# Head-unit accumulators of a projection stream: two PSUM banks moved from the stream's pool to the side pool

## The chip, the cores and the metric

The kernel runs on one core of one Trainium2 chip. The metric is device time in microseconds (us); three runs of the kernel before gave 840.37 us as their median, from 839.36 to 842.27.

## The reference, cut to what matters

One layer of a recurrent decoder is computed for 256 prompt positions and 8 sample positions, together T = 264 columns. All projections are one product `p = x @ w_in` with d_model 2048; its first 2048 columns ("qk") pass through a causal convolution of width 4 and a SiLU:

```
p = x @ w_in
(qk_pre, a_v, a_i, a_f, a_o, a_z, b_q, b_k, b_v, b_g, b_z, g_a, g_b) = _split_cols(p)
ext = jnp.concatenate([conv_buf.astype(qk_pre.dtype), qk_pre], axis=1)
conv = conv_b
for j in range(CONV_W):
    conv = conv + ext[:, j:j + L] * conv_w[j]
qk = jax.nn.silu(conv)
```

The rest (an mLSTM branch, a GLA branch, their norms and gates, two branch projections, the output projection and a LayerNorm) follows later in the stream and is not touched here.

## The kernel before

**Units.** The weight columns are cut into units of 128 columns. Units 0 to 15 are the qk columns, then come the gate columns ("small") and all other projections, the branch projections and the output projection. A unit is a product of 16 blocks of 128 rows, and each block takes three matmuls of 128x264: high part of x by high part of the weight (L218), low part of x by high part of the weight (L219), high part of x by low part of the weight (L221). A unit thus takes 48 matmuls, which accumulate in one PSUM bank.

**Weights.** A unit's weights come as two pieces of 512 KB. In this text pieces are counted from the first unit behind the head: unit 3 takes pieces 0 and 1, unit 4 takes 2 and 3, unit 5 takes 4 and 5, unit 6 takes 6 and 7. A piece is loaded by SP's queue into one of four `raw` buffers (L182), cast by ACT into one of five `hi` buffers (L204), and subtracted by DVE into one of five `lo` buffers (L205). The cast of piece n needs the `hi` buffer of piece n-5 back from TensorE, and the load of piece n the `raw` buffer of piece n-4 back from DVE.

**The head.** Units 0 to 2 (HU = 3) are computed together, block by block, while x itself arrives (nine steps of one or two blocks), so they hold three accumulators at once. From unit 3 on, the units run one after the other.

**Banks.** PSUM's eight banks are two pools: `ps_m` with three, which the stream's units take in turn (tile name `mm`), and `ps_s` with five, which everything else takes in turn (tile name `sd`). A unit's bank is taken from the one that used it three allocations earlier, and its first matmul waits until that tile has been read for the last time.

**Eviction of a qk unit** (`e_qk`, number c): ACT scales the accumulator into `cacc` (L255), DVE adds three shifted products of the same accumulator to it (L257, widths 255, 254, 253, with L259 for the sample columns between), ACT copies eleven columns to `co` (L260) and takes a sigmoid (L261), DVE multiplies (L262). L260 is the last reader of the bank.

**Order.** TensorE's order is that of the code. On ACT and DVE a scheduler sets the order from priorities and its own times, so a dependence that changes in the code can move instructions there; each engine then runs its list in order. Behind unit 4's weights SP also loads five constants (L1162), `wgu_sb` among them, which ACT casts to `wgh` (L301) and DVE turns into `wgr` (L302).

Of the kernel before, what the change touches and what calls it, by code (L numbers as in the profile page):

```python
# [13 lines left out]
F32 = mybir.dt.float32  # L14
# [9 lines left out]
T = L + NB  # L24
# [24 lines left out]
HU = 3  # L49
# [35 lines left out]
def body(ctx, tc, xT, whead, wbig, wsmall, par, cmask, lmask, rowc, gate, wgu, cT, sT, nst, cst, lnr,  # L85
# [11 lines left out]
    ps_m = ctx.enter_context(tc.tile_pool(name="ps_m", bufs=3, space=PSUM))  # L97
# [3 lines left out]
    def t4(shape, name, dt=F32):  # L101
        return b4.tile(shape, dt, tag="b4", name=name)
# [21 lines left out]
    def side_ps():  # L124
        return ps_s.tile([128, 512], F32, tag="sd", name="sd")
# [44 lines left out]
    def load_raw():  # L170

        i = nxt["dma"]
        if i >= len(pieces):
            return
        r = wraw_p.tile([128, KR, 128], F32, tag="raw", name="raw")
        o = 0
        while i < len(pieces) and o + pieces[i][2] <= KR:
            n, k, m, bi = pieces[i]
            w = 128 if bi is not None else SMALL
            src = wbig[bi] if bi is not None else wsmall  # L180
            raws[i] = r[:, o:o + m, 0:w]
            nc.sync.dma_start(out=raws[i], in_=src[:, k:k + m, :])  # L182
            o += m
            i += 1
        nxt["dma"] = i

    def cast_piece():
        i = nxt["cast"]
        while nxt["dma"] <= i:
            load_raw()  # L190
        n, k, m, bi = pieces[i]
        nxt["cast"] += 1
        r = raws.pop(i)
        h = whi_p.tile([128, KR, 128], F32R, tag="hi", name="hi")[:, 0:m]
        if bi is None:
            w = SMALL
            A.copy(out=h[:, :, 0:w], in_=r)
            V.tensor_tensor(out=h[:, :, w:2 * w], in0=r, in1=f(h[:, :, 0:w]), op=ALU.subtract)
            for q in range(m):
                his[n, k + q] = h[:, q, 0:2 * w]  # L200
            return
        lo = wlo_p.tile([128, KR, 128], F32R, tag="lo", name="lo")[:, 0:m]
        with tc.high_priority(offset=PRIO):
            A.copy(out=h, in_=r)  # L204
            V.tensor_tensor(out=lo, in0=r, in1=f(h), op=ALU.subtract)  # L205
        for q in range(m):
            his[n, k + q], los[n, k + q] = h[:, q], lo[:, q]

    def split(hi, lo, src):
        A.copy(out=hi, in_=src)  # L210
        V.tensor_tensor(out=lo, in0=src, in1=f(hi), op=ALU.subtract)

    def products(out, n, k, rhs, start, stop, base=0):

        small = UN[n][0] == "small"
        wh = his[n, k]
        rh, rl = rhs(k - base)
        PE.matmul(out, lhsT=wh, rhs=rh, start=start, stop=False)  # L218
        PE.matmul(out, lhsT=wh, rhs=rl, start=False, stop=small and stop)  # L219
        if not small:  # L220
            PE.matmul(out, lhsT=los[n, k], rhs=rh, start=False, stop=stop)  # L221

    def group(n, k0, k1, rhs, base=0):

        ps = ps_m.tile([128, 512], F32, tag="mm", name="mm")
        out = ps[0:2 * SMALL if UN[n][0] == "small" else 128, 0:T]
        for k in range(k0, k1):
            products(out, n, k, rhs, k == k0, k == k1 - 1, base)
        return ps[:, 0:T]
# [346 lines left out]
    def e_plain(ps, j, key, scale=None):  # L576
        if j == 0:
            st[key] = t4([128, H, T], key)
        A.activation(out=st[key][:, j, :], in_=ps, func=AF.Copy, scale=1.0 if scale is None else scale)
        if j == 3:  # L580
            st[key + "_done"] = True
# [270 lines left out]
    def e_pab(pa, pb, j):  # L852
        g = gtiles[j // 2]
        i = 2 * (j % 2)
        ga, gb = g[:, i, :], g[:, i + 1, :]
        V.tensor_tensor(out=ga, in0=ga, in1=pa, op=ALU.mult)
        V.tensor_tensor(out=gb, in0=gb, in1=pb, op=ALU.mult)
        V.tensor_tensor(out=ga, in0=ga, in1=gb, op=ALU.add)
        split(mh.t(j), ml.t(j), ga)
# [4 lines left out]
    def ln_pre(j):  # L864

        xt = tmp.tile([128, T], F32, tag="t1", name="xt", bufs=T1_BUFS)
        G.tensor_tensor(out=xt, in0=f(x_hi[j // 4][:, j % 4, :]), in1=f(x_lo[j // 4][:, j % 4, :]), op=ALU.add)
        ln["x", j] = xt
# [41 lines left out]
    def ln_shift(j):  # L910

        xt = ln["x", j]
        V.scalar_tensor_tensor(out=xt, in0=xt, scalar=ALPHA, in1=ln["c"], op0=ALU.mult, op1=ALU.subtract)
# [145 lines left out]
    def add(g, front=False):  # L1059
        side.insert(0, g) if front else side.append(g)  # L1060
# [52 lines left out]
    with tc.manual_schedule(engines=MANUAL):  # L1113
        V.memset(ones, 1.0)
        warm = side_ps()
        head = [(side_ps() if u == 0 else ps_m.tile([128, 512], F32, tag="mm", name="mm"))[:, 0:T] for u in range(HU)]
        V.memset(inv256, 1.0 / 256.0)
        V.memset(eps_c, EPS)
        V.memset(one_c, 1.0)
        for _ in range(8):  # L1120
            PE.matmul(warm[:, 0:128], lhsT=ones, rhs=ones, start=True, stop=True)
        k0 = 0
        for m in HEAD:
            k1, i, o = k0 + m, k0 // 4, k0 % 4
            xr = t4([128, m, T], "xr")
            nc.sync.dma_start(out=xr, in_=xT[:, k0:k1, :])
            wr, wh, wl = (p.tile([128, KR, 128], dt, tag=t, name=t)[:, 0:HU * m].rearrange("p (k u) c -> p k u c", u=HU)
                          for p, dt, t in ((wraw_p, F32, "raw"), (whi_p, F32R, "hi"), (wlo_p, F32R, "lo")))
            nc.sync.dma_start(out=wr, in_=whead[:, k0:k1])
            split(x_hi[i][:, o:o + m], x_lo[i][:, o:o + m], xr)  # L1130
            split(wh, wl, wr)
            for u in range(HU):
                for k in range(k0, k1):
                    his[u, k], los[u, k] = wh[:, k - k0, u], wl[:, k - k0, u]
                    products(head[u], u, k, x_rhs, k == 0, k == KT - 1)
            k0 = k1
        nc.sync.dma_start(out=par_sb, in_=par)
        nc.sync.dma_start(out=cst_sb, in_=cst)
        for n, (kind, j) in enumerate(UN):
            st['n'] = n  # L1140
            while nxt["cast"] < min(last.get(n, -1) + 1 + LA, len(pieces)):
                cast_piece()
                while nxt["dma"] < min(nxt["cast"] + RAW_BUFS - 1, len(pieces)):
                    load_raw()
            if kind == "pab":
                pa = group(n, 0, 8, lambda k: (st["yah"].t(k), st["yal"].t(k)))
                pb = group(n, 8, 16, lambda k: (st["ybh"].t(k), st["ybl"].t(k)), base=8)
                e_pab(pa, pb, j)
            elif kind == "out":
                ln_pre(j)  # L1150
                if j >= 8:
                    ln_shift(j)
                ps = group(n, 0, 16, lambda k: (mh.t(k), ml.t(k)))
                e_out(ps, j)
            else:
                ps = head[n] if n < HU else group(n, 0, 16, x_rhs)
                if n == 0:
                    g_conv_prep()
                if n == 4:
                    V.tensor_copy(out=im_sb, in_=ident)  # L1160
                    for dst, src in ((gate_sb, gate), (wgu_sb[64:112], wgu), (rc_sb, rowc), (cm_sb, cmask), (lm_sb, lmask)):
                        nc.sync.dma_start(out=dst, in_=src)  # L1162
                if kind == "qk":
                    for _ in e_qk(ps, j):
                        pass
                elif kind == "small":
                    add(g_gates(ps), True)
                elif kind == "av":
                    e_v(ps, j, "avt", "avd")
                elif kind == "bv":  # L1170
                    e_v(ps, j, "bvt", "bvd")
                elif kind == "bq":
                    e_plain(ps, j, "gq", Q_SCALE)
                elif kind == "bk":
                    e_plain(ps, j, "gk")
                elif kind in ("ao", "az"):
                    e_raw(ps, 2 * j + (kind == "az"), "ozr", 4, g_oz)
                elif kind == "bz":
                    e_raw(ps, j, "bzr", 4, g_bz)
                elif kind in ("ga", "gb"):  # L1180
                    e_raw(ps, 2 * j + (kind == "gb"), "gr", 4, g_g)
            pump(BUDGET)
            if kind == "gb" and j == 15:
                drain()
        ln_final()
# [136 lines left out]
```

## Time and profile before

| | us |
|---|---|
| median of three runs (range) | 840.37 (839.36 to 842.27) |
| the profiled execution | 837.3 |
| its span, first to last instruction | 835.5 |
| TensorE busy in it | 819.5 (98%) |
| DVE busy | 595.0 (71%) |
| ACT busy | 446.5 (53%) |

A busy share is a mean over the whole span; matmuls are pipelined, so a matmul's length in a row (0.28 us) is more than the distance to the next one (0.12 us). What an engine waited for is told by the waits, and the lists of instructions in order of time show where it did.

### The profile page before, as it was taken

The numbers are of one execution on the slowest core, as the hardware profiler recorded it, in microseconds if no ns is written. First come the engines' busy times: TensorE is split into PE (matmuls) and PEld (weight loads), VectorE is DVE, ScalarE is ACT, GpSimd is POOL, SyncE is SP. The second block draws the span as 40 slices with busy tenths as digits, with TensorE's granted clock in tenths as the row PEclk, the third lists the DMA queues.
The fourth block names the chain that finished last, engine by engine and source line by source line (L and its number), as shares of the span: only waits on it lengthen the run. The fifth ranks groups of instructions, "written<-read, shape, count | busy, mean of one in ns | idle before, by whom it ended". The sixth has DMA issues, their size and how long they took to land.

```text
span 835.5 us, 16720 instructions
## 1 busy us (share of the span) xinstructions
PE 819.5 (98%) x6762; PEld 809.9 (97%) x6762; DVE 595.0 (71%) x976; ACT 446.5 (53%) x675; POOL 44.6 (5%) x75
## 2 busy tenths in 40 slices
PE   8799999999999999999999999999999999999996
PEld 8799999999999999999999999999999999999995
DVE  6777667655667787867667997798845777666962
ACT  6555467546455564554546866566544444444633
POOL 0000000000000000001000000012000000000311
PEclk9999999999999999999999999999999999999999
DMA  8756565768759985588888679977655565576513
GB/s 308 253 167 185 158 195 169 202 205 262 247 160 315 310 309 188 200 285 285 278 264 300 200 263 339 296 276 227 197 181 180 183 187 179 180 252 205 186 42 105
DMA packets 56406, 186.39 MB, mean 223 GB/s; under 512 B 8404, under 2 KB 9880, under 8 KB 56328
## 3 DMA queue, kind: packets, MB, share of 16 engines
q1 hardware_dynamic: 52200, 170.90, 62.9%
q0 software_dynamic: 4128, 14.42, 4.5%
q8 instruction: 53, 0.87, 0.4%
q14 instruction: 25, 0.20, 0.1%
HBM read 168.58 MB, written 16.71 MB: 222 GB/s over the span
## 4 chain that ended last, share of the span: by engine, by line
PE 95%; DVE 2%; DMA 2%; ACT 1%; issue 0%; SPq 0%; ACTq 0%; POOLq 0%; POOL 0%; DVEq 0%
PE mm L218 29%; PE mm L219 29%; PE mm L221 29%; DMA gak<-rows_d 1%; PE sd L704 1%; PE sd L466 1%; DMA raw<-whead 1%; PE sd L425 1%; DVE lo L205 1%; PE sd L406 0%; PE sd L440 0%; PE sd L755 0%; PE sd L998 0%; PE sd L221 0%; PE sd L966 0%
## 5 line engine op out<-in xcount | busy, mean ns | idle before, releaser
L218 PE MATMUL mm<-xh,hi 128*128 128x264 f32 (+1 forms) x1536 | 441.1, 288 | 5.3 <-ACT co L260 5.3
L219 PE MATMUL mm<-xl,hi 128*128 128x264 f32 (+1 forms) x1536 | 435.3, 284 | 0.0
L221 PE MATMUL mm<-xh,lo 128*128 128x264 f32 x1520 | 431.0, 284 | 0.0
L204 ACT CAST hi<-raw 128x1024 fp32r<-128x1024 f32 x250 | 261.4, 1047 | 279.3 <-PE mm L219 239.6
L205 DVE TENSOR_TENSOR lo<-raw,hi 128x1024 fp32r<-128x1024 f32 x250 | 307.1, 1230 | 115.0 <-ACT hi L204 110.7
L218 PEld LDWEIGHTS mm<-xh,hi 128*128 128x128 f32 (+1 forms) x1536 | 289.7, 189 | 6.6 <-ACT co L260 5.5
L219 PEld LDWEIGHTS mm<-xl,hi 128*128 128x128 f32 (+1 forms) x1536 | 289.9, 189 | 0.2
L221 PEld LDWEIGHTS mm<-xh,lo 128*128 128x128 f32 x1520 | 285.7, 188 | 0.0
L218 PE MATMUL mm<-mh,hi 128*128 128x264 f32 x256 | 72.7, 284 | 0.0
L221 PE MATMUL mm<-mh,lo 128*128 128x264 f32 x256 | 72.6, 284 | 0.0
L219 PE MATMUL mm<-ml,hi 128*128 128x264 f32 x256 | 72.4, 283 | 0.0
L219 PEld LDWEIGHTS mm<-ml,hi 128*128 128x128 f32 x256 | 48.2, 188 | 0.0
L218 PEld LDWEIGHTS mm<-mh,hi 128*128 128x128 f32 x256 | 48.1, 188 | 0.0
L568 DVE SCALAR_TENSOR_TENSOR cch<-kq,avd,cch 128x256 f32<-128x256 f32 x64 | 29.2, 482 | 26.6 <-DMA kq<-kq_d 24.4
L221 PEld LDWEIGHTS mm<-mh,lo 128*128 128x128 f32 x256 | 48.0, 187 | 0.0
L553 ACT ACTIVATE cch<-cch,decb 128x512 f32<-128x512 f32 x32 | 21.6, 717 | 28.5 <-DMA cch<-cT 28.5
L219 PE MATMUL mm<-ybl,hi 128*128 128x264 f32 x128 | 36.4, 284 | 0.0
L218 PE MATMUL mm<-ybh,hi 128*128 128x264 f32 x128 | 36.4, 284 | 0.0
L218 PE MATMUL mm<-yah,hi 128*128 128x264 f32 x128 | 36.3, 284 | 0.0
L219 PE MATMUL mm<-yal,hi 128*128 128x264 f32 x128 | 36.3, 284 | 0.0
L221 PE MATMUL mm<-yah,lo 128*128 128x264 f32 x128 | 36.2, 283 | 0.0
L221 PE MATMUL mm<-ybh,lo 128*128 128x264 f32 x128 | 36.2, 283 | 0.0
(330 smaller groups left out, 854.3 us busy)
## 6 DMA issues: line engine op xcount, KB each, us to landing
raw<-wbig SPq DMA_DIRECT2D x250, 512.0 KB, 4.7
cch<-cT SPq DMA_DIRECT2D x16, 512.0 KB, 6.1
kq<-kq_d SPq DMA_DIRECT2D x16, 512.0 KB, 7.3
sC<-cch POOLq DMA_DIRECT2D x16, 512.0 KB, 4.9
sch<-sT SPq DMA_DIRECT2D x8, 512.0 KB, 8.5
gak<-rows_d SPq DMA_DIRECT2D x8, 512.0 KB, 7.5
sS<-sch POOLq DMA_DIRECT2D x8, 512.0 KB, 6.9
raw<-whead SPq DMA_DIRECT2D x7, 384.0 KB, 5.5
```

What stands on the lines that cost most here:

```text
L204: A.copy(out=h, in_=r)
L205: V.tensor_tensor(out=lo, in0=r, in1=f(h), op=ALU.subtract)
L218: PE.matmul(out, lhsT=wh, rhs=rh, start=start, stop=False)
L219: PE.matmul(out, lhsT=wh, rhs=rl, start=False, stop=small and stop)
L221: PE.matmul(out, lhsT=los[n, k], rhs=rh, start=False, stop=stop)
L425: PE.matmul(S[:, o:o + n], lhsT=kT.t(2 * h + d)[:, s0:s0 + 128], rhs=qT.t(2 * h + d)[:, t0:t0 + n], start=(d == 0), stop=(d == 1))
L466: PE.matmul(CN[:, 0:VC], lhsT=kw[:, s, d * 128:d * 128 + 128], rhs=vt[h // 2][:, s, h % 2, :], start=(s == 0), stop=(s == 1))
L553: A.activation(out=chunks[i][:, b], in_=chunks[i][:, b], func=AF.Copy, scale=decb[:, h, b0 + b:b0 + b + 1])
L568: V.scalar_tensor_tensor(out=c[:, b, e], in0=r[:, 0, b], scalar=avd[:, j, b0 + b:b0 + b + 1], in1=c[:, b, e], op0=ALU.mult, op1=ALU.add)
L704: PE.matmul(pl[s0:s0 + m, 4 * hf + h, n0:n0 + w].rearrange("p (n s) -> p n s", s=hs), lhsT=K[:, h, hf * 128 + s0:hf * 128 + s0 + m], rhs=r ...
```

## The change

All three accumulators of the head units are taken from the side pool `ps_s`; before, unit 0's was, and those of units 1 and 2 were from `ps_m`.

```diff
-        head = [(side_ps() if u == 0 else ps_m.tile([128, 512], F32, tag="mm", name="mm"))[:, 0:T] for u in range(HU)]
+        head = [side_ps()[:, 0:T] for u in range(HU)]
```

Matmuls, loads and computations are the same in number and size. The lists of TensorE, SP and POOL keep their order; on TensorE only the tile under units 1 and 2 has another name (`sd_108`, `sd_109` for `mm_108`, `mm_109`). Before, the allocations in `ps_m` were those two and then units 3, 4, 5, 6 (`mm_433`, `mm_504`, `mm_582`, `mm_653`), so unit 4 took unit 1's bank, unit 5 unit 2's and unit 6 unit 3's. Now units 3, 4 and 5 take three fresh banks, and unit 6 takes unit 3's as before.

On ACT the scheduler moves casts. From the cast of piece 6 on, before and then now (`hi_498` is piece 6, `hi_570` 7, `hi_576` 8, `hi_641` 9, `hi_647` 10; the three L260 read the banks of units 1, 2 and 3 for the last time):

```order
L204 CAST hi_498<-raw_425 128x1024
L260 COPY co_388<-mm_108 128x11
L261 ACTIVATE csg_402<-cacc_401 128x264
L255 ACTIVATE cacc_411<-mm_109,par_sb_84 128x264
L260 COPY co_388<-mm_109 128x11
L261 ACTIVATE csg_412<-cacc_411 128x264
L255 ACTIVATE cacc_482<-mm_433,par_sb_84 128x264
L301 CAST wgh_1478<-wgu_sb_89 48x512
L204 CAST hi_570<-raw_431 128x1024
L260 COPY co_388<-mm_433 128x11
```

```order
L204 CAST hi_570<-raw_431 128x1024
L260 COPY co_388<-sd_108 128x11
L261 ACTIVATE csg_402<-cacc_401 128x264
L255 ACTIVATE cacc_411<-sd_109,par_sb_84 128x264
L204 CAST hi_576<-raw_496 128x1024
L260 COPY co_388<-sd_109 128x11
L261 ACTIVATE csg_412<-cacc_411 128x264
L255 ACTIVATE cacc_482<-mm_433,par_sb_84 128x264
L301 CAST wgh_1478<-wgu_sb_89 48x512
L204 CAST hi_641<-raw_502 128x1024
L204 CAST hi_647<-raw_574 128x1024
L260 COPY co_388<-mm_433 128x11
```

The casts of pieces 7 to 10 stand earlier among the evictions: the last reader of unit 3's bank stood behind the cast of piece 7, and stands behind that of piece 10 now.

On DVE, around the eviction of unit 3 (`mm_433` is its bank, `cacc_482` its result), before and then now:

```order
L257 SCALAR_TENSOR_TENSOR cacc_482<-mm_433,par_sb_84,cacc_482 128x255
L259 TENSOR_TENSOR cacc_482<-cacc_482,dtap_382 128x8
L302 SCALAR_TENSOR_TENSOR wgr_1479<-wgh_1478,par_sb_84,wgu_sb_89 48x512
L257 SCALAR_TENSOR_TENSOR cacc_482<-mm_433,par_sb_84,cacc_482 128x254
L257 SCALAR_TENSOR_TENSOR cacc_482<-mm_433,par_sb_84,cacc_482 128x253
L205 TENSOR_TENSOR lo_571<-raw_431,hi_570 128x1024
```

```order
L302 SCALAR_TENSOR_TENSOR wgr_1479<-wgh_1478,par_sb_84,wgu_sb_89 48x512
L257 SCALAR_TENSOR_TENSOR cacc_482<-mm_433,par_sb_84,cacc_482 128x254
L205 TENSOR_TENSOR lo_642<-raw_502,hi_641 128x1024
L257 SCALAR_TENSOR_TENSOR cacc_482<-mm_433,par_sb_84,cacc_482 128x253
L205 TENSOR_TENSOR lo_648<-raw_574,hi_647 128x1024
```

Before, the two L257 of this unit followed each other behind L302; now the subtraction of piece 9 (`lo_642`) stands between them. Some fifteen rows further on the lists of ACT and DVE are again those of before, to their ends.

## Rows read from the trace of the kernel before

**Rows 1.** The page: busy us, share and count of TensorE; chain by engine.

```profile
PE 819.5 (98%) x6762; PEld 809.9 (97%) x6762; DVE 595.0 (71%) x976; ACT 446.5 (53%) x675; POOL 44.6 (5%) x75
...
PE 95%; DVE 2%; DMA 2%; ACT 1%; issue 0%; SPq 0%; ACTq 0%; POOLq 0%; POOL 0%; DVEq 0%
```

**Rows 2.** Waits of TensorE, whole span: total us, times, longest us.

```profile
PE mm L218 <- ACT co L260: 5.3, 1, 5.3
PE sd L218 <- ACT hi L210: 1.4, 2, 0.9
...
PE sd L644 <- DVE ns L637: 0.3, 1, 0.3
```

**Rows 3.** Timeline of TensorE: start us, length us, instruction, idle before it.

```profile
9.48 0.39 PE L218 MATMUL sd<-xh,hi 128*128 128x264 f32 x1 [0.88 <-ACT hi L210]
...
25.67 0.28 PE L218 MATMUL mm<-xh,hi 128*128 128x264 f32 x1
...
31.35 0.28 PE L221 MATMUL mm<-xh,lo 128*128 128x264 f32 x1
36.93 0.59 PE L218 MATMUL mm<-xh,hi 128*128 128x264 f32 x1 [5.29 <-ACT co L260]
37.31 0.42 PE L219 MATMUL mm<-xl,hi 128*128 128x264 f32 x1
...
39.92 0.29 PE L219 MATMUL mm<-xl,hi 128*128 128x264 f32 x1
```

**Rows 4.** Windows: stretch, length, busy us by engine, granted clock (1.00 is full), DMA.

```profile
9.40:10.50 1.10, 0.53 (x3) 0.32 (x3) 1.04 (x2) 0.69 (x3) 0.00 (x0) 1.00 1.09 387
...
36.00:36.30 0.30, 0.00 (x0) 0.00 (x0) 0.30 (x2) 0.00 (x0) 0.00 (x0) 1.00 0.84 328
36.30:36.60 0.30, 0.00 (x0) 0.00 (x0) 0.30 (x2) 0.00 (x0) 0.00 (x0) 0.73 0.49 96
36.60:36.90 0.30, 0.00 (x0) 0.00 (x0) 0.14 (x2) 0.20 (x2) 0.00 (x0) 0.50 0.37 96
```

**Rows 5.** Timeline of ACT, from the cast of piece 6.

```profile
33.97 1.04 ACT L204 CAST hi<-raw 128x1024 fp32r<-128x1024 f32 x1 [0.60 <-DMA raw<-wbig]
36.70 0.17 ACT L260 COPY co<-mm 128x11 f32<-128x11 f32 x1 [1.69 <-DVE cacc L257]
...
41.41 0.62 ACT L301 CAST wgh<-wgu_sb 48x512 fp32r<-48x512 f32 x1 [1.15 <-DMA wgu_sb<-wgu]
42.05 1.05 ACT L204 CAST hi<-raw 128x1024 fp32r<-128x1024 f32 x1
43.88 0.17 ACT L260 COPY co<-mm 128x11 f32<-128x11 f32 x1 [0.77 <-DVE cacc L257]
...
47.14 1.05 ACT L204 CAST hi<-raw 128x1024 fp32r<-128x1024 f32 x1 [1.35 <-PE mm L219]
```

**Rows 6.** Timeline of DVE: the subtractions of pieces 3 and 5 to 7, and evictions.

```profile
29.01 1.22 DVE L205 TENSOR_TENSOR lo<-raw,hi 128x1024 fp32r<-128x1024 f32 x1
...
33.54 1.22 DVE L205 TENSOR_TENSOR lo<-raw,hi 128x1024 fp32r<-128x1024 f32 x1
34.67 0.48 DVE L257 SCALAR_TENSOR_TENSOR cacc<-mm,par_sb,cacc 128x254 f32<-128x254 f32 x1
35.06 1.22 DVE L205 TENSOR_TENSOR lo<-raw,hi 128x1024 fp32r<-128x1024 f32 x1
...
42.06 0.75 DVE L302 SCALAR_TENSOR_TENSOR wgr<-wgh,par_sb,wgu_sb 48x512 fp32r<-48x512 f32 x1 [1.21 <-ACT wgh L301]
42.84 1.00 DVE L257 SCALAR_TENSOR_TENSOR cacc<-mm,par_sb,cacc 128x254 f32<-128x254 f32 x2
```

**Rows 7.** Loads of pieces 9 and 10, then all weight loads: issue to landing.

```profile
L182 SPq DMA_DIRECT2D raw<-wbig x2: 328/349/370, 34.8 to 37.8; - x2
...
DMA to landing us min/median/max: 5.6/5.9/6.2
...
DMA to landing us min/median/max: 2.7/4.7/12.1
```

## The prediction, made before the changed kernel was run

> **What bounds the kernel now.** The page comes first: TensorE is busy 98% of the span and the chain that ended last is 95% TensorE [rows 1]. So only what stops or slows TensorE can move the time. Next, what TensorE waited for in the whole span: one single wait of 5.3 us for L260 on ACT leads the list, the second line is two waits of the head's start-up, and the list ends at 0.3 us [rows 2]. Its place is in the timeline [rows 3]: unit 3 starts at 25.67 and its 48th matmul at 31.35, so a matmul takes 5.68 / 47 = 0.121 us and a unit 5.80 us. Unit 4 could start at 31.47 and starts at 36.93. The reason is the bank: unit 4 accumulates where unit 1 did, and the last read of unit 1, the copy to `co`, runs at 36.70 to 36.87 [rows 5]. It is not the weights: piece 3, the second of unit 4, is subtracted by 29.01 + 1.22 = 30.23 [rows 6].
>
> The wait costs more than its length. Last, the granted clock: full until 36.3, 0.50 from 36.6 on [rows 4], that is 1.2 GHz instead of 2.4. From 36.93 to 39.92 stand 13 distances between matmuls [rows 3]; at 0.121 they would take 1.57 us, they took 2.99. So the stall cost 36.93 - 31.47 = **5.46 us** and the slow clock behind it **1.42 us**, together **6.88 us**.
>
> **What the change removes.** Unit 4's first matmul has no earlier user of its bank, and unit 5's neither. Unit 4 starts at 31.47, and with that the clock has no reason to fall. Weights: unit 5 runs from 37.27 on pieces 4 and 5, and piece 5 is subtracted by 33.54 + 1.22 = 34.76 [rows 6]. So 6.88 us go, if nothing else becomes late.
>
> **What it adds.** The next user of an occupied bank is unit 6, on unit 3's. Without a wait it would start at 31.47 + 2 x 5.80 = 43.07. In the trace of before the last read of unit 3 ends at 43.88 + 0.17 = 44.05 [rows 5], already later than that; and the lists of ACT and DVE have changed ahead of it. I replay both lists as they now stand, with lengths and distances from the rows. Until 36.70 little differs: unit 1's eviction is bound by DVE as before. Piece 7's cast finds its `hi` buffer (piece 2's) free at the half of unit 4, 34.4, and comes behind the cast at 33.97.
>
> - `wgh` (L301) waits for a constant that lands at 41.41, as before, since SP's list is unchanged and what stands ahead of it there depends on the subtraction of piece 5, which doesn't move. It ends at 42.03 [rows 5].
> - ACT's next is the cast of piece 9: 42.05 to 43.10 (1.05) [rows 5]. Its load was issued at 34.8 and took 6.2 [rows 7], so it is there at 41.0.
> - DVE: `wgr` at 42.06, the second L257 of unit 3 at 42.84, and 0.39 later (from 34.67 to 35.06 [rows 6]) it is free, at 43.23. Then the subtraction of piece 9, which takes 34.67 - 33.54 = 1.13 to the next start [rows 6]: 44.36. Then the third L257 of unit 3, 0.48 long: 44.84.
> - ACT meanwhile casts piece 10. That cast waits for unit 5's last matmul to give back piece 5's buffer (43.07 and some 0.2 for its end; the row at 47.14 [rows 5] shows such a wait) and for its load (37.8 + 5.6 = 43.4 [rows 7]). It runs from 43.45, and ACT is free for the next at 44.4.
> - `co` of unit 3 then runs at 44.86 to 45.03, and TensorE follows 0.06 later, as at 36.87 and 36.93: unit 6 starts at 45.09.
>
> So a new stall of **2.0 us** stands ahead of unit 6. From below it is bounded by the cast of piece 10, which stands ahead of the copy and needs the end of unit 5 whatever DVE does: 43.07 + 0.2 + 0.94 + 0.17 + 0.06 = 44.44, a stall of 1.4. From above: each microsecond by which piece 10's load or `wgh`'s constant lands later is added; the spread of the two weight loads there is 0.6 [rows 7], so 2.6. I take 2.0, since every term of it is a row of the same microseconds.
>
> What does such a stall do to the clock? Two rows stand on its two sides: after an idle of 0.88 us at 9.48 [rows 3] the window around it shows 1.00 [rows 4], and in the long wait the clock fell only between 36.3 and 36.6, some 4.9 us behind the last matmul. 2.0 is nearer to the first, so I take nothing; the other bound is the 1.42 us measured. The Trainium skill, "TensorE: Matmul & The Clock Gate", section "A second HAM failure mode: psum-queue depth-cycling", says that a kernel that goes round its PSUM banks can let TensorE idle briefly between groups so often that its clock drops and recovers again and again. By that page the stall at unit 6 could cost up to the whole 1.42 more and leave a gain of 3.5; the full clock after the 0.88 idle speaks for one brief idle being harmless, and no run here shows one of 2 us.
>
> **Behind unit 6.** Unit 7 takes unit 4's bank at 45.09 + 5.80 = 50.89. Unit 4's `co` stands behind one cast, that of piece 11, which needs piece 6's buffer at unit 6's half, 48.0, so it is done near 49.2: 1.7 us to spare. Unit 8 at 56.7 needs unit 5's `co`, behind the cast of piece 12, near 52.2. From there the casts wait on TensorE again, as in the row at 47.14 [rows 5], the lists are those of before, and everything to the end is what it was, earlier by one constant. The side banks under units 1 and 2 cost nothing: they are read for the last time near 40, and the side work asks for its first bank only behind the gate unit, thirteen units after unit 3. Behind the head's start-up and this stall TensorE waited once more, for 0.3 us at L644 [rows 2], so nothing there swallows a shift that all engines share.
>
> **Sum.** 5.46 + 1.42 - 2.0 = **4.88 us** gained. The profiled execution took 837.3 us, 1.8 more than its span; it would take 832.4. Its time lies 3.1 below the median of the three runs; against that median, 840.37 - 4.88 = **835.5**. 0.3% of the time, 2.5 us, is about what a measurement of this kernel can tell from no change.
>
> **Rivals.**
> 1. *The clock falls in the new stall.* For it: the only other stall over 1 us did lower it. Against: that took 4.9 us of idleness. The gain is 4.88 - 1.42 = 3.46: 836.9.
> 2. *No new stall.* Whoever reads only the waits of before expects all 6.88: 833.5. For it: the bank was the only wait of note. Against: the floor of 1.4 above, which needs no more than that ACT runs its list in order.
> 3. *The gain is given back later.* The 5.46 us of stall were also time in which loads and casts got ahead; if a later unit found its weights late, or a chain of side work that runs at its own pace stopped TensorE, most of the 4.88 would return as a wait: about 839.5, within 0.3%. Against: unit 6 and 7 have their pieces (9 by 44.4, needed near 53.8), and casts wait for TensorE again soon after, so the lead is limited by buffers and not by the time before.
> 4. *Slower: piece 10 lands late.* Its cast now stands ahead of unit 3's `co`, so a late load holds TensorE's bank, which it didn't before. Unit 6 starts 1.17 us after the landing (0.94 + 0.17 + 0.06). A wait of 5.46 us with the same slow clock behind it would use up the whole gain: a landing at 43.07 + 5.46 - 1.17 = 47.4, 9.5 us after the issue at 37.8. That load took 5.6, and the longest of all took 12.1 [rows 7]; with 12.1 it lands at 49.9, the wait is 8.0, and the time is 840.37 - 6.88 + 8.0 + 1.42 = 842.9.
>
> **How the numbers follow.** Forecast, with a stall of 1.4 to 2.6: 0.72, its own range 834.9 to 836.1 and a microsecond either way for the scatter of medians (the three runs lie 1.0 below to 1.9 above theirs). Rival 1: 0.12. Rival 2: 0.05. Rival 3: 0.08. Rival 4: 0.03. The range reaches from rival 2 to rival 1 with some scatter, 833.3 to 837.5, and leaves out rivals 3 and 4 and the tails. Faster by over 0.3% (below 837.85): the forecast and rivals 1 and 2 but for some 0.04 of scatter, 0.85; within 0.3%: 0.12; slower: 0.03.
>
> **What the profile of the changed kernel would show.** Right: TensorE goes from unit 3 to unit 4 near 31.5 without a gap; the wait of `mm` for `co` on L260 is still in the list, but 1.4 to 2.6 us long, ahead of the 145th matmul behind 25.67 and near 43; the windows from 31 to 60 show a clock of 1.00; the span is near 830.6. Wrong in a step: a distance of 0.22 us between the matmuls behind that wait (rival 1); no such wait (rival 2); a new line among TensorE's waits behind 60 us (rival 3); the cast of piece 10 waiting for its load by several us (rival 4). If the wait there is above 2.6 us, the replay of ACT and DVE is wrong in the step whose start differs.

## The result, and the profile after

| | before | after |
|---|---|---|
| median of five runs, us | 840.37 (839.36 to 842.35) | 835.80 (835.10 to 837.38) |
| ratio, with its 95% interval | | 0.9943 (0.9922 to 0.9963) |
| the profiled execution, us | 837.3 | 837.4 |
| its span, us | 835.5 | 835.6 |

The change makes the kernel 4.6 us faster, and the interval of the ratio leaves out 1; the forecast was 835.5 and 4.88 us. But the two profiled executions are equally long: the one of before was the fastest seen of before, the one of after the slowest of the first five of after. So the two traces can't be subtracted as wholes; they have to be compared stretch by stretch, and one more execution of each kernel has to say what belongs to the change.

Waits of TensorE in the changed kernel, whole span (total, times, longest, in us):

```profile
PE mm L218 <- ACT co L260: 3.2, 1, 3.2
PE sd L218 <- ACT hi L210: 1.8, 2, 1.5
...
PE sd L704 <- DVE gq L711: 0.2, 1, 0.2
```

The first line answers to the first of [rows 2]: the wait for a bank is still there, 3.2 us instead of 5.3. The timeline of TensorE says where:

```profile
27.43 0.28 PE L218 MATMUL mm<-xh,hi 128*128 128x264 f32 x1
...
33.23 0.28 PE L218 MATMUL mm<-xh,hi 128*128 128x264 f32 x1
...
44.71 0.28 PE L221 MATMUL mm<-xh,lo 128*128 128x264 f32 x1
48.15 0.39 PE L218 MATMUL mm<-xh,hi 128*128 128x264 f32 x1 [3.16 <-ACT co L260]
...
48.63 0.42 PE L218 MATMUL mm<-xh,hi 128*128 128x264 f32 x1
...
51.93 0.33 PE L218 MATMUL mm<-xh,hi 128*128 128x264 f32 x1
52.09 0.28 PE L219 MATMUL mm<-xl,hi 128*128 128x264 f32 x1
```

Against [rows 3]: unit 4 follows unit 3 without a gap (27.43 + 5.80 = 33.23), where it waited 5.46 us. Unit 6 could start at 27.43 + 3 x 5.80 = 44.83 and starts at 48.15, a stall of **3.32 us**. From 48.63 to 51.93 the matmuls are 0.22 us apart instead of 0.12; the 19 distances from 48.15 to 52.09 took 3.94 us and should take 19 x 0.121 = 2.30, so the slow clock costs **1.64 us**. And everything is 1.8 us late from the start, since unit 3 starts at 27.43 and not at 25.67. The windows (length, busy us by engine, granted clock, DMA):

```profile
9.00:12.00 3.00, 1.78 (x9) 1.58 (x10) 2.47 (x4) 2.58 (x4) 0.00 (x0) 0.84 1.02 401
12.00:15.00 3.00, 3.00 (x17) 3.00 (x17) 2.81 (x5) 2.51 (x4) 0.00 (x0) 0.59 1.02 367
...
47.50:48.10 0.60, 0.00 (x0) 0.00 (x0) 0.60 (x3) 0.17 (x2) 0.00 (x0) 1.00 0.24 96
48.10:48.40 0.30, 0.25 (x2) 0.25 (x3) 0.30 (x1) 0.30 (x3) 0.00 (x0) 1.00 0.00 0
48.60:51.80 3.20, 3.20 (x17) 3.20 (x16) 2.21 (x7) 0.29 (x1) 0.00 (x0) 0.50 0.81 250
```

Two slow stretches: one in the head, from 11 to 14.4 us, which the trace of before does not have, and one that begins not in the stall but half a microsecond behind it: the clock is full to its end and in the first matmuls of unit 6, and 1.2 GHz from 48.6 on. In [rows 4] the clock had fallen inside the wait.

ACT's list ahead of the new stall, against [rows 5]:

```profile
41.96 1.05 ACT L204 CAST hi<-raw 128x1024 fp32r<-128x1024 f32 x1 [2.03 <-DMA raw<-wbig]
42.92 0.16 ACT L260 COPY co<-sd 128x11 f32<-128x11 f32 x1
...
43.89 0.62 ACT L301 CAST wgh<-wgu_sb 48x512 fp32r<-48x512 f32 x1
44.53 1.05 ACT L204 CAST hi<-raw 128x1024 fp32r<-128x1024 f32 x1
45.80 1.04 ACT L204 CAST hi<-raw 128x1024 fp32r<-128x1024 f32 x1 [0.22 <-DMA raw<-wbig]
47.93 0.17 ACT L260 COPY co<-mm 128x11 f32<-128x11 f32 x1 [1.09 <-DVE cacc L257]
```

These are the steps of the forecast in their order: `wgh`, the cast of piece 9, that of piece 10, the copy of unit 3 behind DVE's third L257, and TensorE 0.05 us behind the copy's end. Counted from unit 3's start the copy begins 1.3 us later than forecast (47.93 - 27.43 = 20.50, forecast 44.86 - 25.67 = 19.19). The first row is why: the cast of piece 8 waited 2.03 us for its load and began 41.96 - 27.43 = 14.53 us behind unit 3's start, where the load's landing in the trace of before allows 38.9 - 25.67 = 13.2. The load of piece 8 from issue to landing, before and then now:

```profile
raw<-wbig SPq DMA_DIRECT2D x1, 512.0 KB, 5.6
```

```profile
raw<-wbig SPq DMA_DIRECT2D x1, 512.0 KB, 6.9
```

DVE's subtraction of piece 8 waits for that cast, and behind it on DVE's list, without a gap, stand unit 2's L262, unit 3's first L257 and L259, and then `wgr` (L302):

```profile
43.04 1.23 DVE L205 TENSOR_TENSOR lo<-raw,hi 128x1024 fp32r<-128x1024 f32 x1 [1.02 <-ACT hi L204]
...
45.11 0.75 DVE L302 SCALAR_TENSOR_TENSOR wgr<-wgh,par_sb,wgu_sb 48x512 fp32r<-48x512 f32 x1
```

So `wgr` starts 17.68 us behind unit 3's start, where the forecast had 42.06 - 25.67 = 16.39. `wgh` had ended 0.6 us before it: at the last, `wgr` waited for DVE's own list.

### The profile page after: what moved, and what is told of

Its sections match the earlier page's. It is cut to its first block, busy times and chain, and to the rows that moved or that the text cites. A ratio compares the mean times of both kernels' runs of the same rounds, so it can differ in the third digit from the quotient of the medians.

```text
span 835.6 us, 16720 instructions
## 1 busy us (share of the span) xinstructions
PE 821.0 (98%) x6762; PEld 811.0 (97%) x6762; DVE 594.0 (71%) x976; ACT 446.2 (53%) x675; POOL 43.7 (5%) x75
## 4 chain that ended last, share of the span: by engine, by line
PE 90%; DVE 4%; DMA 4%; issue 1%; ACT 1%; SPq 0%; ACTq 0%; POOLq 0%; POOL 0%; DVEq 0%
PE mm L218 27%; PE mm L219 27%; PE mm L221 27%; DMA kq<-kq_d 2%; DVE lo L205 1%; PE sd L466 1%; DMA raw<-wbig 1%; PE sd L704 1%; PE sd L221 1%; DMA raw<-whead 1%; PE sd L218 1%; PE sd L219 1%; PE sd L425 1%; DVE scr L570 1%; PE sd L440 0%
## 5 line engine op out<-in xcount | busy, mean ns | idle before, releaser
L218 PE MATMUL mm<-xh,hi 128*128 128x264 f32 (+1 forms) x1504 | 431.9, 288 | 3.2 <-ACT co L260 3.2
L219 PE MATMUL mm<-xl,hi 128*128 128x264 f32 (+1 forms) x1504 | 426.3, 284 | 0.0
L221 PE MATMUL mm<-xh,lo 128*128 128x264 f32 x1488 | 422.0, 284 | 0.0
L205 DVE TENSOR_TENSOR lo<-raw,hi 128x1024 fp32r<-128x1024 f32 x250 | 307.2, 1231 | 111.5 <-ACT hi L204 109.2
L218 PEld LDWEIGHTS mm<-xh,hi 128*128 128x128 f32 (+1 forms) x1504 | 283.6, 189 | 4.5 <-ACT co L260 3.4
L219 PEld LDWEIGHTS mm<-xl,hi 128*128 128x128 f32 (+1 forms) x1504 | 283.9, 189 | 0.2
L221 PEld LDWEIGHTS mm<-xh,lo 128*128 128x128 f32 x1488 | 279.8, 188 | 0.0
L553 ACT ACTIVATE cch<-cch,decb 128x512 f32<-128x512 f32 x32 | 21.6, 717 | 37.4 <-DMA cch<-cT 37.4
```

What stands on the lines that cost most here:

```text
L553: A.activation(out=chunks[i][:, b], in_=chunks[i][:, b], func=AF.Copy, scale=decb[:, h, b0 + b:b0 + b + 1])
```

## The experiments

Each run is compared with runs of the kernel before on the same chip; times are medians.

**E1, the changed kernel once more** (no edit).

> The changed kernel once more. Its first profile has two things that the prediction did not: the head ended 1.8 us later than in the trace of before, with a clock of one half from 11 to 14.4 us, and the wait ahead of unit 6 was 3.2 us instead of 2.0, with a slow clock behind it. Theory: the late head belongs to the execution (loads of x and of the head's weights that land later), not to the change, which does not touch the first 25 us; then a repeat can show unit 3 starting near 25.7 again, and the time stays at 835 to 837. Rival: the head's banks in the side pool slow it; then every profile shows unit 3 starting 1.5 us or more later than 25.67.

Measured: 835.15 us (nine runs, 832.56 to 838.88) against 839.70; ratio 0.9952 (0.9933 to 0.9970). Timeline of TensorE in its profile:

```profile
25.08 0.28 PE L218 MATMUL mm<-xh,hi 128*128 128x264 f32 x1
...
44.92 0.39 PE L218 MATMUL mm<-xh,hi 128*128 128x264 f32 x1 [2.28 <-ACT co L260]
45.15 0.28 PE L219 MATMUL mm<-xl,hi 128*128 128x264 f32 x1
45.27 0.28 PE L221 MATMUL mm<-xh,lo 128*128 128x264 f32 x1
```

Unit 3 starts at 25.08, so the rival falls: the side banks don't slow the head. The stall ahead of unit 6 is 44.92 - (25.08 + 17.40) = 2.44 us, and behind it the distances are 0.12 us from the second on: no slow clock. The span is 830.9, 4.6 below that of before's first profile. Neither profile has the slow stretch in the head, but E1's head ends 0.6 us earlier (25.08 against 25.67).

**E8, the kernel before once more** (no edit).

> The kernel before, profiled once more. Theory: the wait of 5.3 us ahead of unit 4 with 1.4 us of slow clock behind it is there in every execution; the slow stretch in the head, which the first profile of before did not have and that of the changed kernel had, is there in some executions of either, so a span of 837 to 840 and a mean clock below 0.996 go with it. Rival (the head is slow only with its banks in the side pool): unit 3 starts at 25.67 again.

Measured: 840.24 us, span 838.5. Timeline and windows of its profile:

```profile
27.48 0.28 PE L218 MATMUL mm<-xh,hi 128*128 128x264 f32 x1
...
38.73 0.59 PE L218 MATMUL mm<-xh,hi 128*128 128x264 f32 x1 [5.29 <-ACT co L260]
39.12 0.42 PE L219 MATMUL mm<-xl,hi 128*128 128x264 f32 x1
...
42.56 0.29 PE L221 MATMUL mm<-xh,lo 128*128 128x264 f32 x1
```

```profile
12.00:14.00 2.00, 2.00 (x11) 2.00 (x11) 1.95 (x4) 1.50 (x3) 0.00 (x0) 0.50 1.01 373
37.00:39.00 2.00, 0.27 (x1) 0.27 (x2) 1.55 (x3) 0.49 (x3) 0.00 (x0) 0.50 0.84 205
```

The slow head is there in the kernel before too: unit 3 starts at 27.48, with a clock of 0.50 between 12 and 14. It belongs to the execution. The wait ahead of unit 4 is the same to a hundredth, 38.73 - (27.48 + 5.80) = 5.45 us, and the 17 distances behind it, to 42.56, took 3.83 us instead of 2.05: 1.78 us of slow clock. So this execution is the one to set beside the first profile of after: both heads slow, spans 838.5 and 835.6, 2.9 us apart.

**E5, the clock's share in the kernel before.**

```diff
+            if n == 4:
+                for _ in range(40):
+                    PE.matmul(warm[:, 0:T], lhsT=x_hi[0][:, 0, 0:128], rhs=x_hi[0][:, 0, :], start=True, stop=True)
```

> The kernel before, with 40 extra matmuls of 128x264 (4.8 us, into a bank nobody reads) between unit 3 and unit 4, inside the wait of 5.46 us. They take no time of their own, since the wait for unit 1's bank ends behind them, but TensorE is not idle in it. Theory: the clock stays full and the 1.42 us behind the wait go: 1.0 to 1.8 us below the kernel before, and distances of 0.12 us between unit 4's first matmuls. Rival (the slow matmuls come from something else, such as the loads of weights): the distances stay at 0.22 and the time is that of before.

Measured: 837.47 us (twelve runs) against 839.65; ratio 0.9970 (0.9955 to 0.9985). Timeline of TensorE:

```profile
32.84 5.01 PE L1147 MATMUL sd<-xh 128*128 128x264 f32 x40
38.29 0.39 PE L218 MATMUL mm<-xh,hi 128*128 128x264 f32 x1 [0.44 <-ACT co L260]
38.51 0.28 PE L219 MATMUL mm<-xl,hi 128*128 128x264 f32 x1
38.64 0.28 PE L221 MATMUL mm<-xh,lo 128*128 128x264 f32 x1
```

The stall is as long as ever (38.29 - 32.84 = 5.45 us), only filled, and the matmuls behind it are 0.12 us apart from the second on. Taking the idleness away without taking the wait away is worth 2.2 us by the medians (1.3 to 3.8 by the interval), where the trace counted 1.42 and, in E8, 1.78. That the stall of before cost more than its length is shown.

**E4, half of the change.**

```diff
-        head = [(side_ps() if u == 0 else ps_m.tile([128, 512], F32, tag="mm", name="mm"))[:, 0:T] for u in range(HU)]
+        head = [(side_ps() if u < 2 else ps_m.tile([128, 512], F32, tag="mm", name="mm"))[:, 0:T] for u in range(HU)]
```

> Half of the change: only unit 1's accumulator moves to the side pool, unit 2's stays in the stream's. Unit 4 finds a fresh bank, unit 5 waits for unit 2's last read. Theory: by the same replay that read is done near 39.9 and unit 5 starts 2.8 us late, with or without a slow clock behind it (1.4): 836 to 838, somewhat slower than the full change and faster than before. Rival (removing the first wait is all that counts, the second bank does nothing): equal to the changed kernel within 0.5 us, and no wait at unit 5.

Measured: 837.33 us (twelve runs) against 839.70; ratio 0.9975 (0.9958 to 0.9992). Timeline of TensorE and two windows:

```profile
41.99 0.59 PE L218 MATMUL mm<-xh,hi 128*128 128x264 f32 x1 [3.00 <-ACT co L260]
```

```profile
41.00:41.90 0.90, 0.00 (x0) 0.00 (x0) 0.86 (x3) 0.13 (x2) 0.00 (x0) 0.53 0.96 253
44.00:45.00 1.00, 1.00 (x6) 1.00 (x6) 0.95 (x2) 0.00 (x0) 0.00 (x0) 0.50 0.95 328
```

With one bank moved the wait moves to unit 5 and is 3.0 us long. In this profile, of the slowest of the twelve executions (841.68), the clock fell in it and stayed at one half until 47.9: the 26 distances behind the wait, to 47.88, took 5.89 us instead of 3.15, so the slow clock cost 2.7 us. The full change is 2.2 us faster than this half by the medians of the same chip (835.15 in E1). The intervals of the two ratios overlap, so the times alone don't prove that the second bank counts; the wait at unit 5, which the full change doesn't have, does.

**E2, the list behind the new stall.** The five constants are loaded behind unit 8's weights. (On SP's queue they stand behind piece 9, of unit 7, in the kernels before and after, and behind piece 11 here.)

```diff
-                if n == 4:
+                if n == 8:
                     V.tensor_copy(out=im_sb, in_=ident)
```

> The changed kernel with the five constants loaded behind unit 8's weights instead of unit 4's, so that the cast to wgh no longer stands ahead of unit 3's last read on ACT, and only piece 9's cast does (the scheduler now puts piece 10's cast behind it). Theory (the new wait is ACT's and DVE's list): the wait ahead of unit 6 falls from 2 to 3 us to at most 1, the clock stays full behind it, and the time is 1.5 to 4.5 us below the changed kernel's, 831.5 to 834.5. Rival (late loads of pieces 8 and 9 make the wait, not the list): the wait stays above 1.5 us and the time within 1 us of the changed kernel's.

Measured: 832.97 us against 839.70; ratio 0.9921 (0.9906 to 0.9935), 2.2 us below the changed kernel's median on the same chip. ACT's list and TensorE's start of unit 6:

```profile
41.77 1.05 ACT L204 CAST hi<-raw 128x1024 fp32r<-128x1024 f32 x1
43.83 0.17 ACT L260 COPY co<-mm 128x11 f32<-128x11 f32 x1 [1.01 <-DVE cacc L257]
...
44.81 0.62 ACT L301 CAST wgh<-wgu_sb 48x512 fp32r<-48x512 f32 x1
```

```profile
44.05 0.39 PE L218 MATMUL mm<-xh,hi 128*128 128x264 f32 x1 [0.65 <-ACT co L260]
```

`wgh` and the cast of piece 10 now stand behind the copy, and the wait is 0.65 us, with a full clock behind it. Piece 8's load doesn't explain the difference: in E1 piece 8's cast begins 12.9 us behind unit 3's start (37.96 - 25.08), here 12.8 (38.61 - 25.84), and yet unit 3's copy comes 19.6 us behind it in E1 (44.70) and 18.0 here (43.83). What moved is the order on ACT and DVE. A wait of 1.1 us for L205 is in this profile, but it lies between 500 and 600 us, where it is also seen in E1 (0.2), E8 (0.3) and E5 (1.1); it is no consequence of a late unit 6.

**E3, no bank to wait for.**

```diff
-    ps_m = ctx.enter_context(tc.tile_pool(name="ps_m", bufs=3, space=PSUM))
-    ps_s = ctx.enter_context(tc.tile_pool(name="ps_s", bufs=5, space=PSUM))
+    ps_m = ctx.enter_context(tc.tile_pool(name="ps_m", bufs=4, space=PSUM))
+    ps_s = ctx.enter_context(tc.tile_pool(name="ps_s", bufs=4, space=PSUM))
...
-            ps = side_ps() if (t, g) not in ((0, 3), (1, 0), (1, 1)) else ps_m.tile([128, 512], F32, tag="mm", name="zT")
+            ps = side_ps() if (t, g) not in ((0, 2), (0, 3), (1, 0), (1, 1)) else ps_m.tile([128, 512], F32, tag="mm", name="zT")
```

> The changed kernel with four banks for the stream and four for the side work (one more of the last transposes takes a stream bank). ACT's and DVE's lists stay those of the changed kernel, but units 3 to 6 all find fresh banks and unit 7 is the first to wait for unit 3's, which is read by 45 to 48, and needed at 49. Theory: no wait of TensorE for L260 above 0.5 us at all, clock full from the head on, 831 to 834. Rival (the gain is given back, by weights that come late or by side work that is short of banks): new lines among TensorE's waits, time at 835.8 or more.

Measured: 832.92 us (six runs) against 839.70; ratio 0.9922 (0.9901 to 0.9943). Waits of TensorE in its profile, an execution with a slow head and a span of 835.1:

```profile
PE sd L542 <- ACT num L444: 1.7, 1, 1.7
...
PE mm L221 <- DVE lo L205: 0.8, 1, 0.8
PE sd L644 <- DVE ns L637: 0.7, 1, 0.7
```

No wait for L260 is left, and from 16 to 200 us the clock is full. Both sides of the bet show: by the medians the gain is that of E2, and the side work, with a bank less, holds TensorE for 1.7 us at L542, near 206 us. Behind that wait the clock falls once more:

```profile
206.40:209.70 3.30, 3.30 (x16) 3.30 (x16) 3.23 (x13) 0.93 (x4) 0.76 (x2) 0.50 0.86 283
```

That the missing bank makes the wait at L542 is not shown: E10 has the same four and four, and its profile has no such wait.

**E6, the clock behind the new stall.** As in E5, in the changed kernel, `n == 6` and 18 matmuls.

> The changed kernel with 18 such matmuls (2.2 us) ahead of unit 6, inside its wait of 2.0 to 3.3 us. Theory: in the executions where the clock falls around that wait (its first profile; not that of the repeat) it stays full now, so the median falls by a part of 1.42 us, 0.3 to 1.2 below the changed kernel's 835.2 to 835.8, and the profile shows 1.00 from 43 to 60 us. Rival (the clock has nothing to do with the idle time there): no change of the median beyond 0.3, and slow stretches behind unit 6 as often as before.

Measured: 834.00 us (six runs, 832.29 to 834.72) against 839.65; ratio 0.9925 (0.9903 to 0.9946). Timeline of TensorE:

```profile
44.18 2.34 PE L1147 MATMUL sd<-xh 128*128 128x264 f32 x18
46.35 0.28 PE L218 MATMUL mm<-xh,hi 128*128 128x264 f32 x1
46.47 0.29 PE L219 MATMUL mm<-xl,hi 128*128 128x264 f32 x1
```

and the copy of unit 3 on ACT:

```profile
45.98 0.17 ACT L260 COPY co<-mm 128x11 f32<-128x11 f32 x1 [0.53 <-DVE cacc L257]
```

Full clock behind it. Unit 3 starts at 26.78 here, so the copy comes 19.20 us behind it, as forecast (19.19): by that row the stall without the filler would have been some 2.0 us (an estimate: 45.98 + 0.17 + 0.06 - 44.18). The median is 1.2 us below E1's, at the upper end of what was expected, but the intervals of the two ratios overlap, so the direction is supported and the size is not settled.

**E7, the clock in the head.**

```diff
+            for _ in range({1: 4, 2: 10}.get(k0, 0)):
+                PE.matmul(warm[:, 0:T], lhsT=x_hi[0][:, 0, 0:128], rhs=x_hi[0][:, 0, :], start=True, stop=True)
             for u in range(HU):
```

> The changed kernel with 4 and 10 such matmuls ahead of the second and third step of the head, where TensorE waits 0.2 to 1.6 us for the first casts, and where four of six profiles have shown no fall and the others a clock of one half from 11 to 14.4 us. Theory: with less idle time in the first 10 us the clock stays full in the head, unit 3 starts at 25.0 to 26.3 in every execution, and the median falls by 0.5 to 1.5 us with less scatter. Rival (the late head comes from the loads alone): the head ends as late as it did, and the filler costs up to 1 us where the data are early.

(The count in that text is off: of the six profiles until then three had the slow head.) Measured: 834.07 us (six runs, 833.19 to 837.41) against 839.65; ratio 0.9934 (0.9911 to 0.9956). In its profile unit 3 starts at 25.38 and the head's clock is full; the stall ahead of unit 6 is 45.56 - (25.38 + 17.40) = 2.78 us, this time with a clock that is at one half from 45.1 on, inside the wait. (ACT's list is another one here: `wgh`, which waits 1.67 us for its constant, stands ahead of unit 2's copy already.)

```profile
9.00:15.00 6.00, 5.68 (x47) 5.47 (x46) 5.44 (x7) 4.83 (x8) 0.00 (x0) 1.00 1.03 391
45.50:48.30 2.80, 2.74 (x12) 2.74 (x13) 2.71 (x7) 0.80 (x3) 0.00 (x0) 0.50 0.69 224
```

Of the nine profiles without this filler six have the slow head, of the three with it (E9 and E10 are the others) none. The median is 1.1 us below E1's; with intervals that overlap and three profiles, the filler's effect is supported and not shown.

**E9 and E10, together.** E9 is E2's and E7's edits; E10 is E2's, E3's and E7's.

> The changed kernel with the constants loaded behind unit 8's weights and the 4 and 10 extra matmuls in the head. Theory: the two gains lie in different stretches (the wait at unit 6 with what follows it; the clock in the head), so they add: 2.2 to 2.6 us from the first, about 1 from the second, together 831 to 832.5. Rival (the weights of units 6 and 7 then come late and take it back): TensorE waits for L205 by more than 1.5 us in sum and the time is that of the run with later constants alone, 833.

Measured, E9: 832.85 us (six runs, 830.80 to 835.76) against 840.40; ratio 0.9910 (0.9888 to 0.9931). The expected sum was missed, and not for the rival's reason: no wait for L205 is in its profile, but one of 1.6 us for L260. The scheduler had put `wgh` ahead of the copy again:

```profile
40.22 1.05 ACT L204 CAST hi<-raw 128x1024 fp32r<-128x1024 f32 x1
43.45 0.61 ACT L301 CAST wgh<-wgu_sb 48x512 fp32r<-48x512 f32 x1 [2.19 <-DMA wgu_sb<-wgu]
44.09 0.17 ACT L260 COPY co<-mm 128x11 f32<-128x11 f32 x1
```

The cast waits 2.19 us for its constant with TensorE's bank behind it: the same mechanism, here without a wait for DVE. So E9 doesn't test whether the two gains add.

> The same with four banks for the stream and four for the side work. Theory: no wait for L260 at all; what is left are the wait for unit 6's weights (0.8 to 1.1 us) and that of the side work for its fourth bank (1.7 us at L542 in the run with four banks), so 830.5 to 833, equal to the run before within 1 us. Rival (the bank was still what held TensorE): 1 us or more below it.

Measured, E10: 831.30 us (five runs, 830.43 to 832.28) against 840.40; ratio 0.9887 (0.9870 to 0.9904), the fastest version. (The expectation places the L205 waits at unit 6; they lie behind 500 us, see E2.) ACT's list in its profile has `wgh` ahead of unit 3's copy as well, which runs at 45.50, but unit 7 is the first to need that bank, at 25.75 + 4 x 5.80 = 48.95, and TensorE waits for no bank. Neither of the two waits that were expected to be left, for L205 and at L542, is in this profile; 0.9 us at L704 and 1.1 us at L644 are. Between E9 and E10 the extra bank is worth 1.5 us by the medians, which is the rival's side, though the intervals of the two ratios overlap a little.

## Why the prediction was right, point by point

- **What goes.** The wait ahead of unit 4 went wholly, as forecast: 5.46 us in the first trace, 5.45 in E8. The clock behind it was counted at 1.42; E8 has 1.78, and E5 values it at 2.2 (1.3 to 3.8).
- **What comes.** A new stall was forecast ahead of unit 6, with its chain over `wgh`, pieces 9 and 10, DVE's L257 and `co`. The place and the order of the steps are right; E2 and E9 support the chain's order as the cause, since the wait is 0.65 us with `wgh` and piece 10 behind the copy, and 1.6 us with `wgh` ahead of it again. The size was too small: 2.0 forecast, bounded at 2.6, and 3.32 and 2.44 measured in the two executions of the changed kernel (and 2.78 in E7, with its other list). By the prediction's own sign the replay is wrong in the step whose start differs, and that step is `wgr`. It was let start as soon as `wgh`'s constant had landed and was cast, and as late landings the upper bound knew only those of piece 10 and of that constant. The loads and subtractions of pieces 7 and 8, which the new lists put ahead of unit 3's eviction, had no term. In the four profiles that have the forecast's list (us; loads from issue to landing, the rest from unit 3's start):

  | | load of piece 7 | load of piece 8 | start of `wgr` | start of unit 3's copy |
  |---|---|---|---|---|
  | forecast (loads of the trace of before) | 5.3 | 5.6 | 16.39 | 19.19 |
  | E6 | 5.6 | 5.4 | 16.38 | 19.20 |
  | E1 | 6.1 | 5.2 | 16.80 | 19.62 |
  | E3 | 6.3 | 5.7 | 17.04 | 19.87 |
  | first profile of after | 5.8 | 6.9 | 17.68 | 20.50 |

  From `wgr` to the copy it is 2.8 us in every row, as replayed. What differs is how late one of the two loads lands: its subtraction then comes late on DVE, and everything behind it on that list as well. Why these loads take longer in one execution than in another stays open.
- **The clock behind the new stall** was put at nothing, by the row of an idle of 0.88 us. It fell around the stalls of 3.32 and 2.78 us, not around that of 2.44, and cost 1.64 us in the first profile. So rival 1 is what happened there, and its "against", that a fall took 4.9 us of idleness, did not hold. The page of the Trainium skill named there ("TensorE: Matmul & The Clock Gate", "A second HAM failure mode: psum-queue depth-cycling") tells of TensorE idling between groups so frequently that its clock goes down and up again and again. This trace agrees only in part: here a single stall of 2.78 or 3.32 us was enough, and one of 2.44 us was not.
- **The sum** came out closer than its terms, and that is luck in part: too small were the clock behind the old wait on one side, and the new stall and the clock behind it on the other. The stretch from unit 3's start to unit 9's holds both kernels' stalls and the slow clock behind them: it took 41.7 us (first profile) and 42.1 (E8) before, and 39.8 (first profile) and 37.4 (E1) after. The gain there is 3.3 us by the means, 1.9 to 4.7 by the single pairs, where 4.88 was forecast. The medians say 4.6, by the interval 3.1 to 6.6. So 3.3 lies inside the interval, and whether more than scatter stands behind the remaining 1.3 stays open.
- **Rival 2**, no new stall: not seen in the changed kernel; E2 and E3, where little or nothing of the stall is left, are another 2.2 us faster by the medians.
- **Rival 3**, given back later: small waits at L644, L704 and L205 (0.2 to 1.1 us, 2.2 at most in E4) come and go, in before's executions as well. From unit 9's start to the end the four profiles took 768.1 and 768.9 us before and 768.4 and 768.5 after: nothing is given back there.
- **Rival 4**, a late piece 10: in the profiles ACT waited for it 0.2 and 0.6 us. The loads that were late were those of pieces 7 and 8, further ahead in the same list.
- **The base.** The span of before that the sum was made against, 835.5, was a lucky one: it lies 2 to 3 us below the spans that go with the medians, and its head without a slow stretch is 1.8 us of the 3.0 that part it from E8's. Making the sum of differences against the median, not the span, kept the forecast right.

## What to carry to other kernels

A wait for a bank is paid at the next user of that bank: when accumulators get fresh banks, look for the next unit that finds an occupied one, and replay there, from the rows, the in-order lists of the engines that read it last, since whatever stands ahead of that last reader (a cast, a small constant that is still on its way) is now part of TensorE's path. An idle TensorE costs its length and in some executions a slow clock on top (1.4 to 1.8 us in most of the profiles here, 2.7 in E4), so a wait that can't be removed can be made cheaper by work of no use, as in E5. And a single profile is one draw: compare two kernels by stretches that begin alike in both.

## What the runs showed of the hardware

The clock did not fall in the same place in all waits. In the kernel before, the wait ahead of unit 4 is 5.46 us long in the first profile and 5.45 in E8; the clock fell some 4.9 us into the one and 2.4 us into the other (at 35.6). It fell 2.2 us into the wait of 3.0 us in E4 and 2.3 us into that of 2.8 us in E7, and half a microsecond behind the end of the wait of 3.3 us in the first profile of after and of the wait of only 1.7 us at L542 in E3. Around the wait of 2.4 us in E1 it did not fall at all. In the head TensorE waited 1.6 us in two waits for its casts in E2, with a full clock, and 1.1 us in E6, with a slow one. So near these lengths the same idleness is free in one execution and costs 1.4 to 1.8 us, in E4 more, in the next. That may be much of the scatter, but the runs don't show it: the changed kernel's nine runs in E1 lie within 6.3 us and E10's five, with no wait for a bank and the filler in the head, within 1.9, yet the changed kernel's first five runs lie within 2.3.
